# Gated layer's second output projection: both column pairs by seven block products, and the last head's root applied by a diagonal matrix in the transposition

## The chip, the core and the metric

The kernel runs on one core of a Trainium2 chip. The metric is the device time in microseconds (us) of one execution, of which the median over several runs is taken. The core has a matrix engine (TensorE: PE in the profile, PEld for its weight loads), VectorE (DVE), ScalarE (ACT), GpSimd (POOL), and a queue engine (SP) that starts most transfers from memory.

## The reference

Two layers with a gated feed path stand one after the other: a gated linear attention layer (4 heads, 1024 value columns each) and a retention layer (8 heads). There are 256 tokens, a model width of 2048 and an inner width of 4096, all in float32. What matters here is the end of the attention layer:

```
o = o * lax.rsqrt(jnp.mean(o * o, axis=-1, keepdims=True) + EPS)     # per token and head
o = o.reshape(B, S, D_INNER).astype(h.dtype) * head_g
return (o * jax.nn.silu(gate)) @ w_out                               # w_out: 4096 x 2048
h = h + gla_mixer(...)                                               # then the retention layer
```

## The kernel before

Every weight is float32 and comes from memory in blocks of 128 x 1024 (512 KB; two row tiles of 512 columns), into buffers called `raw`. A block is then split into two parts that the matrix engine multiplies at full rate: `hi`, a rounded copy made by ACT (L298), and `lo`, the remainder `raw - hi` made by DVE (L299). A product of a row tile of the block with 128 tokens is three matmuls of 512 columns: hi with hi, lo with hi, hi with the activations' lo part (`three`, L408; `mm3`, L341 to L343). There are four `hi` and four `lo` buffers (L203, L204), and a split is started at most three ahead of the one that PE works on (`LOOK = 3`). What is called a split below has a number in program order (lo216 is the 217th).

Where two groups of 512 output columns use the same left side, the kernel can compute both together for the first half of the rows (kt 0 to 7, for both halves of the tokens) by seven products of blocks in place of eight, in the manner of Strassen and Winograd: `pair` in `_plan` orders loads and splits, and `out_pair` (L985) does the arithmetic. The left sides of four of the products are sums of activations, made by `make_sums` (L441; tiles `osum`). The right sides are sums of weight blocks: some are made by a transfer that adds while it writes (POOL, L310), some by an addition on DVE (L293) just before a split. A product over 4 row tiles is two splits of 6 matmuls each (`product`, L418); the second half of the rows (kt 8 to 15) is done directly for both columns, in splits of 12 matmuls (`direct`, L425). Products `P1` to `P8` and the direct steps `v4` to `v7`, `g4` to `g7` follow one another in the order of a string such as `UNIT`. `JOINT` (L169) says for each projection which of its two pairs of columns are done this way: for the second half of this layer's projection, `("ao", 1)`, the first pair is not, and its two columns (tiles `gb0`, `gb1`) are 8 direct splits each; the second pair (tiles `gbe2`) is.

The left side of this projection, `ogt`, is written by `og_part` (L880) for each of a head's two groups of 512 columns: the head's root `hr` is formed from the sums of squares `sso` by a chain of small DVE instructions (`rsqrt`, Newton steps, L492 to L497), then `o`, `hr` and the gate `sg` are multiplied in one DVE instruction for 128 tokens (L895), `transpose_out` (L701) transposes 128 x 128 blocks by PE against the identity (L707; tiles `got6`, `got7` for the last head), and ACT and DVE split the transposed blocks into `ogt` (L500, L501). The last head (number 3, groups 6 and 7) fills kt 8 to 15 of this half. So kt 0 to 7 are there earlier.

The order of instructions on each engine is set by a scheduler when the program is built: it starts from the order in the code, from priorities (`high_priority`) and from what must stay in order (`keep`), and each engine then runs its list in order. Transfers are issued in order by SP (loads of `raw`) and POOL (adding transfers, and the residual `gb_resid`, 2 MB, L481).

Of the kernel before, what the change touches and what calls it, by code (L numbers as in the profile page):

```python
# [17 lines left out]
P = 128  # L18
# [46 lines left out]
def _plan():  # L65


    loads, subs = [], []

    def load(gid, j):  # L70
        loads.append((gid, j))
        return len(loads) - 1

    def use(c, pre=None, post=()):
        subs.append((c, pre, post))

    def plain(gid, js=range(NSUB)):
        for j in js:
            use(load(gid, j))

    def pair(g, v, q=None, order=None):
        order = (order or UNIT).split()
        x = [load(g, 0), load(g, 1)] if order[0] == "P1" else []
        z = []
        later = max(("P3", "P6"), key=order.index)
        for n, tok in enumerate(order):
            kind, i = tok[0], tok[1:]
            if kind in "qvg":
                plain({"q": q, "v": v, "g": g}[kind], [int(i)])
            elif tok == "z":  # L90
                z += [load(v, 2), load(v, 3)]
            elif tok == "P2":
                plain(g, [2, 3])
            else:
                if tok == "P1" and not x:
                    x += [load(g, 0), load(g, 1)]
                for j in range(2):
                    post = []
                    if tok == later:
                        post.append((z[j], (v, j)))  # L100
                    if tok == "P1":
                        post.append((x[j], (v, j)))
                    if tok == "P6":
                        post.append((x[j], (g, 2 + j)))
                    use(z[j] if tok in ("P3", "P7") else x[j], z[j] if tok == "P6" else None, post)

    def out_cols_of(name, half, cut, joint):
        for c in (0, 2):
            cols = [(name, half, c + n) for n in range(2)]
            if joint[c // 2]:  # L110
                pair(cols[1], cols[0])
# [36 lines left out]
    free = [-1 - n for n in range(NRAW)] + [-1] * len(SPARE)  # L148
    buf = []
    for c in range(len(loads)):  # L150
        b = min([*range(NRAW), *_spare(loads[c])], key=lambda n: free[n])
        buf.append(b)
        free[b] = last[c]
    return loads, subs, places, last, buf


UNIT = "P1 v4 z P3 v5 P5 v6 P6 P2 v7 P7 g4 g5 P8 g6 g7"
MIXED = "q0 q1 P1 q2 q3 q4 z P5 q5 P6 q6 q7 P2 P3 v4 v5 v6 P7 v7 g4 g5 P8 g6 g7"
WHOLE = " ".join(f"q{j}" for j in range(NSUB)) + " " + UNIT


def ret_order(h):
# [16 lines left out]
def kernel(  # L179
# [261 lines left out]
    def make_sums(lhs, name, where):  # L441
        s = cur["s"] = [None] * 4
# [12 lines left out]
        yield  # L455
        tt(f3, f6, y[1][:, :, one_], ALU.add)
        tt(f7, y[0][:, :, one_], y[0][:, :, two], ALU.subtract)
        yield
        for i, x in ((0, f3), (1, f5), (2, f6), (3, f7)):
            if i % 2 == 0:  # L460
                two_ = room(i // 2)
                s[i], s[i + 1] = two_[:, 0], two_[:, 1]
            keep(nc.scalar.activation(s[i][:, :, 0, :], x, AF.Copy))
            keep(tt(s[i][:, :, 1, :], x, s[i][:, :, 0, :].bitcast(F32), ALU.subtract))
            if i % 2:
                yield
# [234 lines left out]
    def transpose_out(src, kt0, scale0, dst, name):  # L701
        for half in range(2):
            tp = mis_p.tile([P, 2, SEQ], F32, tag="mis", name=f"{name}_tp{half}")
            for jj in range(2):
                j = half * 2 + jj
                for t in range(2):
                    nc.tensor.transpose(  # L707
                        tp[:, jj, t * P : (t + 1) * P], src(t, j), ident
                    )
            kt = kt0 + half * 2  # L710
            with tc.high_priority():
                if scale0 is None:
# [123 lines left out]
    def gla_head(h):  # L836
# [42 lines left out]

        def og_part(gj):  # L880
            g = 2 * h + gj
            if gj == 0:
# [9 lines left out]
            o, sg, hr = os_[gj], sgs[gj], hw["hr"]  # L892
            with tc.high_priority():
                for t in range(2):
                    nc.vector.scalar_tensor_tensor(  # L895
                        o[:, t, :], o[:, t, :], hr[:, t : t + 1], sg[:, t, :], ALU.mult, ALU.mult
                    )
            yield
            yield from transpose_out(
                lambda t, j: o[:, t, j * P : (j + 1) * P],  # L900
# [1 line left out]
                S_HG + 4 * g,  # L902
                ogt,
                f"got{g}",
            )
# [79 lines left out]
    def out_pair(c, first, name, final=False):  # L985
# [36 lines left out]
        g = c + 1  # L1022
        cur["pin"] = final
        product(A, plain(0, 0), stop=True)
        advance()
        direct(lhs, (C, V1), 4)
        join(g, 0, A)
        advance()
        product(C, summed(0))
        advance()  # L1030
        direct(lhs, (C, V1), 5)
        drain_side()
        product(P5, summed(1), stop=True)
        direct(lhs, (C, V1), 6)
        for t in range(2):
            join(c, t, P5)
        product(A, summed(2), stop=True)
        product(B, plain(4, 0))
        join(c, 0, A, ALU.subtract)
        direct(lhs, (C, V1), 7, stop=True)  # L1040
# [26 lines left out]
        if onward:  # L1067
            for _ in late[0]:
                pass
            tasks.append(out_transposes(g))  # L1070
        begun.clear()
        closed.clear()

# [24 lines left out]
    def out_half(first, final, name, cut=0, hook=None, joint=(False, False)):  # L1098
        pend = {}
        for c in range(4):  # L1100
            if joint[c // 2]:
                if c % 2 == 0:
                    out_pair(c, first, name)
                continue
            if cut and c == 0:
                if True:
# [353 lines left out]
    for h in range(2, 4):  # L1460
        gla_head(h)
    get_resid("gb_resid")
    slots = deque((2, 3, 0, 1))
    out_half(False, False, "gb", joint=JOINT["ao", 1])
    put_resid("resid_g")
# [122 lines left out]
```

## Time and profile before

| | |
|---|---|
| median of the three runs | 1374.34 us (1373.69 to 1375.95) |
| time of the profiled execution | 1373.26 us |
| its span, first to last instruction | 1371.5 us |
| PE busy | 1362.3 us, 99% of the span |
| DVE, ACT, POOL busy | 1098.4, 847.0, 136.8 us |
| the last head's group 7 gates end, the projection's first column pair starts | 565.1 us into the span |
| first column pair ends, second begins | 611.4 us |

The span is the time between the first and the last instruction; the execution's own time is 1.76 us longer. Durations below are those of this one execution. A busy time of PE counts each matmul from its start to its end, and matmuls overlap: two of 512 columns start 0.227 us apart and each shows 0.39 us. So waits of PE are read from the distances of the starts. DVE and ACT instructions overlap a little too (0.08 to 0.10 us), so that the distance of starts is again what one costs.

### The profile page before, as it was taken

To read this page: it belongs to the slowest core of one execution; us is meant where nothing else is said; L and a number is where in the kernel's file an instruction comes from. 1 tells how busy PE (TensorE), PEld (TensorE's weight loads), DVE (VectorE), ACT (ScalarE), POOL (GpSimd) and SP (SyncE) were. 2 spreads that over 40 slices of the span, in tenths; PEclk is the share of its full clock that TensorE was granted. 3 is DMA by queue.
4 is the path that set the end of the run, shared out by engine and by line. 5 is a ranking of instruction groups with operands and counts; after the bars stand their busy time and mean duration, and the time that the engine had idled before them with its cause. 6 is when DMAs were issued, how large, how long until landed. Compare 5 with 4: busy or idle time off the path is not lost.

```text
span 1371.5 us, 18372 instructions
## 1 busy us (share of the span) xinstructions
PE 1362.3 (99%) x6564; PEld 1145.0 (83%) x6564; DVE 1098.4 (80%) x1520; ACT 847.0 (62%) x1119; POOL 136.8 (10%) x194
## 2 busy tenths in 40 slices
PE   9999999999999999999999999999999999999997
PEld 8888888888888888888888888888888888888886
DVE  6686795987878896769887988897867897889796
ACT  6576656656567756656666576655546665666565
POOL 1003020110021021001011010100101101010010
PEclk9999999999999999999999999999999999999999
DMA  9755566789658667868897878796798797979773
GB/s 358 259 175 168 169 208 184 156 247 318 200 153 262 204 204 183 319 169 232 267 331 197 260 202 249 207 316 218 172 367 219 240 261 197 259 198 317 241 176 124
DMA packets 84508, 315.04 MB, mean 230 GB/s; under 512 B 9776, under 2 KB 10800, under 8 KB 83136
## 3 DMA queue, kind: packets, MB, share of 16 engines
q1 hardware_dynamic: 67200, 241.63, 50.4%
q0 software_dynamic: 15920, 64.89, 23.9%
q10 hardware_dynamic: 1296, 7.35, 1.4%
q8 instruction: 51, 0.84, 0.2%
q14 instruction: 41, 0.34, 0.1%
HBM read 303.35 MB, written 10.49 MB: 229 GB/s over the span
## 4 chain that ended last, share of the span: by engine, by line
PE 99%; DMA 1%; DVE 0%; ACT 0%; DVEq 0%; issue 0%; ACTq 0%
PE rqk_ps L384 8%; PE re_ps L412 8%; PE re_ps L413 8%; PE re_ps L414 8%; PE rqk_ps L385 4%; PE gqk_ps L384 4%; PE gg_ps L342 3%; PE gv_ps L343 3%; PE gv_ps L341 3%; PE gv_ps L342 3%; PE gg_ps L341 3%; PE gg_ps L343 3%; PE ge_ps L412 2%; PE ge_ps L413 2%; PE ge_ps L414 2%; PE gae_ps L413 2%
## 5 line engine op out<-in xcount | busy, mean ns | idle before, releaser
L299 DVE TENSOR_TENSOR lo<-raw,hi 128x1024 fp32r<-128x1024 f32 (+1 forms) x568 | 687.4, 1221 | 215.5 <-ACT hi L298 205.5
L298 ACT ACTIVATE hi<-raw 128x1024 fp32r<-128x1024 f32 (+1 forms) x568 | 595.9, 1055 | 394.3 <-DMA raw<-in_w_all 50.8
L384 PE MATMUL rqk_ps<-xhl,hi 128*128 128x512 f32 x480 | 162.9, 397 | 0.0
L413 PE MATMUL re_ps<-lo,xhl 128*128 128x512 f32 x352 | 137.5, 391 | 0.0
L414 PE MATMUL re_ps<-hi,xhl 128*128 128x512 f32 x352 | 137.3, 390 | 0.0
L310 POOL DMA_DIRECT2D raw<-in_w_all x90 | 78.0, 868 | 556.1 <-DVE lo L299 222.1
L412 PE MATMUL re_ps<-hi,xhl 128*128 128x512 f32 x352 | 132.6, 391 | 0.0
L385 PE MATMUL rqk_ps<-xhl,lo 128*128 128x256 f32 x480 | 122.5, 281 | 0.0
L384 PEld LDWEIGHTS rqk_ps<-xhl,hi 128*128 128x128 f32 x480 | 89.7, 188 | 17.8
L385 PEld LDWEIGHTS rqk_ps<-xhl,lo 128*128 128x128 f32 x480 | 87.6, 189 | 3.4
L414 PEld LDWEIGHTS re_ps<-hi,xhl 128*128 128x128 f32 x352 | 66.1, 188 | 13.6
L413 PEld LDWEIGHTS re_ps<-lo,xhl 128*128 128x128 f32 x352 | 66.2, 188 | 13.2
L412 PEld LDWEIGHTS re_ps<-hi,xhl 128*128 128x128 f32 x352 | 66.0, 188 | 13.2
L384 PE MATMUL gqk_ps<-xhl,hi 128*128 128x512 f32 x216 | 76.6, 399 | 0.0
L342 PE MATMUL gg_ps<-lo,xhl 128*128 128x512 f32 x192 | 75.5, 393 | 0.0
L342 PE MATMUL gv_ps<-lo,xhl 128*128 128x512 f32 x192 | 75.3, 392 | 0.0
L341 PE MATMUL gv_ps<-hi,xhl 128*128 128x512 f32 x192 | 75.2, 393 | 0.0
L343 PE MATMUL gv_ps<-hi,xhl 128*128 128x512 f32 x192 | 75.1, 391 | 0.0
L343 PE MATMUL gg_ps<-hi,xhl 128*128 128x512 f32 x192 | 75.0, 391 | 0.0
L341 PE MATMUL gg_ps<-hi,xhl 128*128 128x512 f32 x192 | 74.9, 392 | 0.0
L829 POOL TENSOR_TENSOR s<-s,m 128x64 f32<-128x64 f32 x56 | 36.1, 676 | 232.5 <-DVE m L820 223.2
L385 PE MATMUL gqk_ps<-xhl,lo 128*128 128x256 f32 x216 | 59.1, 281 | 0.0
(434 smaller groups left out, 2659.8 us busy)
## 6 DMA issues: line engine op xcount, KB each, us to landing
raw<-in_w_all SPq DMA_DIRECT2D x449, 512.0 KB, 4.9
raw<-in_w_all POOLq DMA_DIRECT2D x90, 512.0 KB, 6.8
resid<-in_x_n SPq DMA_DIRECT2D x2, 1024.0 KB, 10.8
gg<-in_gn_g POOLq DMA_DIRECT2D x8, 256.0 KB, 4.2
resid_x<-resid ACTq DMA_DIRECT2D x1, 2048.0 KB, 7.9
gb<-in_gn_b POOLq DMA_DIRECT2D x8, 256.0 KB, 6.0
gb_resid<-resid_x POOLq DMA_DIRECT2D x1, 2048.0 KB, 11.3
resid_g<-gb_resid ACTq DMA_DIRECT2D x1, 2048.0 KB, 10.5
```

Source lines behind the costliest of these rows:

```text
L298: a = nc.scalar.activation(hi[:, sl], src[:, sl], AF.Copy)
L299: b = nc.vector.tensor_tensor(lo[:, sl], src[:, sl], hi[:, sl].bitcast(F32), ALU.subtract)
L310: nc.gpsimd.dma_start(raws[n], block(key), accum_op=ALU.add)
L341: pin(mm(ps, xh, hi[:, q, :], start=kt == 0, stop=False, **onto))
L342: pin(mm(ps, xh, lo[:, q, :], start=False, stop=False, **onto))
L343: pin(mm(ps, xl, hi[:, q, :], start=False, stop=kt == end - 1, **onto))
L384: mm(ps[c], wh, rhs[:, kt, :, :], start=kt == 0, stop=False)
L385: mm(ps[c][:, 0, :], wl, rhs[:, kt, 0, :], start=False, stop=False)
L412: pin(mm(ps, xh, hi[:, q, :], start=start, stop=False, **again))
L413: pin(mm(ps, xh, lo[:, q, :], start=False, stop=False, **again))
L414: pin(mm(ps, xl, hi[:, q, :], start=False, stop=stop, **again))
L829: nc.gpsimd.tensor_tensor(dst, dst, side_of(m[:, li, :], z), ALU.add)
```

## The change

The first pair of columns of `("ao", 1)` is done by seven products as well (`JOINT`), in an order of its own, `LATE`, which puts products that need only kt 0 to 7 ahead of the direct steps. The sums of activations are made during the last head (`make_sums(..., "next_s")`, stepped in `joint_turn`). In the last head, `o` is multiplied by the gate alone, as soon as the gate is there; the root goes into two diagonal matrices `hd` (the identity with each row times `hr`, DVE), and the transposition becomes an ordinary float32 matmul of `o` with `hd`. `out_pair` gets a second order of steps (`late_direct`).

```
-    ("ao", 1): (False, True),
+    ("ao", 1): (True, True),
...
+LATE = "P1 P2 z P3 v4 P5 v5 P6 v6 v7 P7 g4 g5 P8 g6 g7"
...
-                    nc.tensor.transpose(
-                        tp[:, jj, t * P : (t + 1) * P], src(t, j), ident
-                    )
+                    to = tp[:, jj, t * P : (t + 1) * P]
+                    if diag is None:
+                        nc.tensor.transpose(to, src(t, j), ident)
+                    else:
+                        mm(to, src(t, j), diag[:, t, :], start=True, stop=True)
...
+            scaled = h == GLA_H - 1
+            if scaled and gj == 0:
+                hw["diag"] = sc_p.tile([P, 3, P], F32, tag="s32", name=f"hd{h}", bufs=1)
+            if scaled:
+                with tc.high_priority():
+                    for t in range(2):
+                        nc.vector.tensor_tensor(o[:, t, :], o[:, t, :], sg[:, t, :], ALU.mult)
...
+                    if scaled:
+                        for t in range(2):
+                            nc.vector.tensor_scalar(hw["diag"][:, t, :], ident, hr[:, t : t + 1], None, ALU.mult)
...
+        making = make_sums(ogt, "osum2", sums_in_v, "next_s") if h == 3 else None
...
+            if making and tok in ("P3", "P5", "P6", "v7", "g6"):
+                next(making)
...
         product(A, plain(0, 0), stop=True)
...
+        if late_direct:
+            product(B, plain(4, 0))
+            join(g, 0, A)
+            product(C, summed(0))
+            while len(side) > 1:
+                advance()
+            advance()
+            direct(lhs, (C, V1), 4)
+            advance()
+            product(P5, summed(1), stop=True)
+            advance()
+            direct(lhs, (C, V1), 5)
+            for t in range(2):
+                join(c, t, P5)
+            drain_side()
+            product(A, summed(2), stop=True)
+            direct(lhs, (C, V1), 6)
+            join(c, 0, A, ALU.subtract)
+            direct(lhs, (C, V1), 7, stop=True)
...
+                    out_pair(c, first, name, late_direct=c == 0 and name == "gb")
```

On DVE, in the first microseconds of the projection, the list before reads so (hr3 is the last head's root, go6 and go7 its two groups, lo219 to lo221 are the splits of direct steps 3 to 5 of the first column):

```order
L497 SCALAR_TENSOR_TENSOR hr3_4993<-hr3_nw_4996 128x2
L895 SCALAR_TENSOR_TENSOR go6_4710<-go6_4710,hr3_4993,gsg6_4650 128x512 x2
L895 SCALAR_TENSOR_TENSOR go7_4945<-go7_4945,hr3_4993,gsg7_4654 128x512
L299 TENSOR_TENSOR lo219_5038<-raw187_4844,hi219_5037 128x1024
L895 SCALAR_TENSOR_TENSOR go7_4945<-go7_4945,hr3_4993,gsg7_4654 128x512
L299 TENSOR_TENSOR lo220_5065<-raw188_4856,hi220_5064 128x1024
L299 TENSOR_TENSOR lo221_5092<-raw189_4877,hi221_5091 128x1024
L501 SCALAR_TENSOR_TENSOR ogt_106<-got6_tp0_5053,smalls_102,ogt_106 128x256
L501 SCALAR_TENSOR_TENSOR ogt_106<-got6_tp1_5080,smalls_102,ogt_106 128x256
```

and at the same place now, from the join of the first product to the splits of P6 (hd3 are the diagonal matrices; raw184 += raw188 and raw185 += raw189 are the weight sums for splits 226 and 227):

```order
L1018 TENSOR_TENSOR gb_resid_5056<-gbe0_ps1_5059,gb_resid_5056 128x512
L497 TENSOR_TENSOR hr3_nw_5021<-hr3_nw_5021 128x2
L300 TENSOR_TENSOR lo223_5110<-raw184_4824,hi223_5109 128x1024
L300 TENSOR_TENSOR lo224_5121<-raw185_4826,hi224_5120 128x1024
L498 SCALAR_TENSOR_TENSOR hr3_5018<-hr3_nw_5021 128x2
L300 TENSOR_TENSOR lo225_5161<-raw191_4965,hi225_5160 128x1024
L294 TENSOR_TENSOR raw184_4824<-raw184_4824,raw188_4866 128x1024
L294 TENSOR_TENSOR raw185_4826<-raw185_4826,raw189_4892 128x1024
L903 TENSOR_SCALAR hd3_4990<-ident_103,hr3_5018 128x128 x2
L300 TENSOR_TENSOR lo226_5188<-raw184_4824,hi226_5187 128x1024
L300 TENSOR_TENSOR lo227_5200<-raw185_4826,hi227_5199 128x1024
```

The multiplication of go6 and go7 has gone up the list (go6 into the seven products of group 7), the diagonals stand behind two splits of the weights and two additions, and the splits 226 and 227 behind them.

On PE, the transpositions of group 6 stood within the third direct split of column 0 (tiles gb0):

```order
L341 MATMUL gb0_ps1_5034<-hi218_5010,ogt_106 128x512
L342 MATMUL gb0_ps1_5034<-lo218_5011,ogt_106 128x512
L707 MATMUL got6_tp0_5053<-ident_103,go6_4710 128x128
L707 MATMUL got6_tp1_5080<-ident_103,go6_4710 128x128
L343 MATMUL gb0_ps1_5034<-hi218_5010,ogt_106 128x512
L707 MATMUL got6_tp0_5053<-ident_103,go6_4710 128x128 x3
L707 MATMUL got6_tp1_5080<-ident_103,go6_4710 128x128 x3
L341 MATMUL gb0_ps0_5033<-hi218_5010,ogt_106 128x512
L342 MATMUL gb0_ps0_5033<-lo218_5011,ogt_106 128x512
L343 MATMUL gb0_ps0_5033<-hi218_5010,ogt_106 128x512
```

and stand now behind four products, within the first split of `P6` (lo226; tile gbe0_p5 is the bank of `P5`):

```order
L414 MATMUL gbe0_p5_5062<-lo224_5121,osum20_4883 128x512
L415 MATMUL gbe0_p5_5062<-hi224_5120,osum20_4883 128x512
L413 MATMUL gbe0_ps1_5059<-hi226_5187,osum21_5012 128x512
L712 MATMUL got6_tp0_5130<-hd3_4990,go6_4710 128x128
L712 MATMUL got6_tp1_5139<-hd3_4990,go6_4710 128x128
L712 MATMUL got6_tp0_5130<-hd3_4990,go6_4710 128x128 x3
L712 MATMUL got6_tp1_5139<-hd3_4990,go6_4710 128x128 x3
L414 MATMUL gbe0_ps1_5059<-lo226_5188,osum21_5012 128x512
L415 MATMUL gbe0_ps1_5059<-hi226_5187,osum21_5012 128x512
L413 MATMUL gbe0_ps1_5059<-hi226_5187,osum21_5012 128x512
```

PE's list now has P1, P2, P3, P5 and one matmul of P6 ahead of the first transposition, 49 matmuls, where 29 of the projection stood before; the direct step v4 (split 222) comes only behind split 227's first matmul.

On POOL, the transfers that add weight blocks followed on the residual's load for the second pair only (raw200 to raw204):

```order
L481 DMA gb_resid_5031<-resid_x_2994 128x4096
L310 DMA raw200_5163<-in_w_all 128x1024
L310 DMA raw201_5181<-in_w_all 128x1024
L310 DMA raw203_5225<-in_w_all 128x1024
L310 DMA raw204_5252<-in_w_all 128x1024
L310 DMA raw200_5163<-in_w_all 128x1024
L310 DMA raw201_5181<-in_w_all 128x1024
```

and now come for both pairs; raw184 and raw185 are written again for `P5`, raw188 and raw189 for `P7`, raw184 and raw185 once more for `P8`:

```order
L482 DMA gb_resid_5056<-resid_x_2994 128x4096
L311 DMA raw184_4824<-in_w_all 128x1024
L311 DMA raw185_4826<-in_w_all 128x1024
L311 DMA raw188_4866<-in_w_all 128x1024
L311 DMA raw189_4892<-in_w_all 128x1024
L311 DMA raw184_4824<-in_w_all 128x1024
L311 DMA raw185_4826<-in_w_all 128x1024
```

Six adding transfers are new on POOL, and SP has two loads fewer (448 for 450). In all there are 576 splits for 570.

More of the change, by code (lines that the diff above doesn't have):

```diff
@@ L110, in out_cols_of @@
             if joint[c // 2]:
-                pair(cols[1], cols[0])
+                pair(cols[1], cols[0], order=LATE if cols[0] == ("ao", 1, 0) else None)
                 continue
@@ L439, in sums_in_v, with make_sums @@
         return lambda n: v_p.tile([P, 2, QK, 2, P], F32R, tag="v", name=f"{name}{n}")
-    def make_sums(lhs, name, where):
-        s = cur["s"] = [None] * 4
+    def make_sums(lhs, name, where, key="s"):
+        s = cur[key] = [None] * 4
         room = where(name)
@@ L699, in o_mms, with transpose_out @@
                 mm(ps[t], al, v[:, s, 0, :], start=False, stop=end)
-    def transpose_out(src, kt0, scale0, dst, name):
+    def transpose_out(src, kt0, scale0, dst, name, diag=None):
         for half in range(2):
@@ L881, in og_part @@
             g = 2 * h + gj
+            o, sg = os_[gj], sgs[gj]
+            scaled = h == GLA_H - 1
[5 more added lines that the diff above has]
+                        nc.vector.tensor_tensor(o[:, t, :], o[:, t, :], sg[:, t, :], ALU.mult)
             if gj == 0:
@@ L889, in og_part @@
                     rsqrt(hr, m, 2, f"hr{h}")
+                    if scaled:
+                        for t in range(2):
+                            nc.vector.tensor_scalar(hw["diag"][:, t, :], ident, hr[:, t : t + 1], None, ALU.mult)
                 hw["hr"] = hr
                 yield
[L892 to L897, printed above, removed]
+            hr = hw["hr"]
+            if not scaled:
+                with tc.high_priority():
+                    for t in range(2):
+                        nc.vector.scalar_tensor_tensor(
+                            o[:, t, :], o[:, t, :], hr[:, t : t + 1], sg[:, t, :], ALU.mult, ALU.mult
+                        )
             yield
@@ L983, in tail_banks, with out_pair @@
         return ps
-    def out_pair(c, first, name, final=False):
+    def out_pair(c, first, name, final=False, late_direct=False):
         lhs, s = ogt, cur["s"]
@@ L1024, in out_pair @@
         product(A, plain(0, 0), stop=True)
[L1025 to L1040, printed above, removed]
+        if late_direct:
[10 more added lines that the diff above has]
+            direct(lhs, (C, V1), 5)
+            for t in range(2):
+                join(c, t, P5)
[4 more added lines that the diff above has]
+            direct(lhs, (C, V1), 7, stop=True)
+        else:
+            advance()
+            direct(lhs, (C, V1), 4)
+            join(g, 0, A)
+            advance()
+            product(C, summed(0))
+            advance()
+            direct(lhs, (C, V1), 5)
+            drain_side()
+            product(P5, summed(1), stop=True)
+            direct(lhs, (C, V1), 6)
+            for t in range(2):
+                join(c, t, P5)
+            product(A, summed(2), stop=True)
+            product(B, plain(4, 0))
+            join(c, 0, A, ALU.subtract)
+            direct(lhs, (C, V1), 7, stop=True)
         product(A, summed(3), stop=True)
@@ L1069, in out_pair @@
                 pass
-            tasks.append(out_transposes(g))
+            (side if c == 0 else tasks).append(out_transposes(g))
         begun.clear()
@@ L1102, in out_half @@
                 if c % 2 == 0:
-                    out_pair(c, first, name)
+                    out_pair(c, first, name, late_direct=c == 0 and name == "gb")
                 continue
@@ L1462 @@
     get_resid("gb_resid")
+    cur["s"] = cur["next_s"]
     slots = deque((2, 3, 0, 1))
```

1 line of the change is left out of this document (added).

## The prediction

> **What bounds the kernel now.** I read the page first: span, busy shares, the chain that ended last.
>
> ```profile
> span 1371.5 us, 18372 instructions
> ...
> PE 1362.3 (99%) x6564; PEld 1145.0 (83%) x6564; DVE 1098.4 (80%) x1520; ACT 847.0 (62%) x1119; POOL 136.8 (10%) x194
> ...
> PE 99%; DMA 1%; DVE 0%; ACT 0%; DVEq 0%; issue 0%; ACTq 0%
> ```
>
> PE is the chain. A busy share of 99% could hide short waits, since matmuls overlap, so the view of waits comes second. These are all that PE has in the whole span:
>
> ```profile
> PE warm_ps L521 <- POOL lnone L523: 1.0, 1, 1.0
> PE zps L640 <- DVE wa L614: 0.4, 1, 0.4
> ```
>
> Both are at the start. So a change can gain only what it takes out of PE's list, and loses whatever it makes PE wait. Third, the stretches around the first column pair, in columns PE, PEld, DVE, ACT, POOL, clock, DMA share, GB/s:
>
> ```profile
> 560.00:570.00 10.00, 10.00 (x46) 8.29 (x45) 9.23 (x22) 6.10 (x9) 0.00 (x0) 1.00 0.85 346
> 570.00:580.00 10.00, 10.00 (x51) 8.30 (x51) 6.66 (x9) 5.00 (x8) 0.00 (x0) 1.00 0.71 212
> 580.00:590.00 10.00, 10.00 (x47) 8.32 (x46) 4.62 (x7) 4.62 (x7) 0.00 (x0) 1.00 0.53 159
> 590.00:600.00 10.00, 10.00 (x49) 8.34 (x49) 7.86 (x10) 6.86 (x12) 0.00 (x0) 1.00 0.60 194
> ```
>
> DVE is 92% busy in the first ten microseconds and then has room: that is the pattern to keep in mind, since a pair by products asks DVE for more, and earliest.
>
> **PE's list: minus 12 matmuls, 16 dearer transpositions.** The first and the 28th of the projection's matmuls in order of time:
>
> ```profile
> 565.06 0.39 PE L341 MATMUL gb_ps<-hi,ogt 128*128 128x512 f32 x1
> 571.18 0.39 PE L341 MATMUL gb_ps<-hi,ogt 128*128 128x512 f32 x1
> ```
>
> 27 steps in 6.12 us are 0.2267 us a matmul. Two columns directly are 16 splits of 12, 192 matmuls; the pair by products is 14 splits of 6 and 8 of 12, 180. That is 12 x 0.2267 = 2.72 us less.
>
> A transposition is one matmul; the float32 product with the diagonal I price by the float32 products of the same shape in the score stage, two records each (4 heads x 7 levels x 2 products are 56, the trace has 112). Rows of the chain, and the group:
>
> ```profile
> 92.54 1.34 PE lv L763 x12
> 153.65 0.87 PE got_tp L707 x8
> L763 PE MATMUL lv<-w 128*128 128x128 f32 x112 | 15.7, 274 | 0.0
> ```
>
> 0.112 us a record, so 0.223 us a product, against 0.109 for a transposition: 16 x 0.114 = 1.83 us more. PE's list gets shorter by 0.89 us, and that is the most that the change can gain with these prices.
>
> [...] The trace's rows put the ratio at 2, and I take the rows.
>
> **The waits: DVE's list from split 218 to P6.** DVE before, in order of time:
>
> ```profile
> 563.64 1.23 DVE L299 TENSOR_TENSOR lo<-raw,hi 128x1024 fp32r<-128x1024 f32 x1 [0.29 <-ACT hi L298]
> 564.78 0.15 DVE L496 TENSOR_TENSOR hr_nw<-hr_nw 128x2 f32<-128x2 f32 x1
> 564.85 0.68 DVE L1401 TENSOR_TENSOR gsg<-ge_ps,gsg 128x512 f32<-128x512 f32 x1
> 565.45 0.15 DVE L497 SCALAR_TENSOR_TENSOR hr_nw<-hr_nw 128x2 f32<-128x2 f32 x1
> 565.63 0.16 DVE L495 SCALAR_TENSOR_TENSOR hr_nw<-hr_nw,hm 128x2 f32<-128x2 f32 x1
> ...
> 566.22 2.08 DVE L895 SCALAR_TENSOR_TENSOR go<-go,hr,gsg 128x512 f32<-128x512 f32 x3
> 568.22 1.22 DVE L299 TENSOR_TENSOR lo<-raw,hi 128x1024 fp32r<-128x1024 f32 x1
> ```
>
> By the distances of starts a split costs DVE 1.14 us, a 128x512 operation 0.60, a small step 0.07 between long ones and 0.18 behind one that it depends on. A direct split feeds PE for 12 x 0.2267 = 2.72 us, a split of a product for 1.36. So in a run of products DVE has 0.22 us beside each split, and the new list puts far more there. ACT before:
>
> ```profile
> 562.54 1.06 ACT L298 ACTIVATE hi<-raw 128x1024 fp32r<-128x1024 f32 x1 [0.78 <-PE ge_ps L414]
> 565.26 0.69 ACT L1403 ACTIVATE gsg<-ge_ps,rr 128x512 f32<-128x512 f32 x1 [1.66 <-PE ge_ps L414]
> 565.85 1.05 ACT L298 ACTIVATE hi<-raw 128x1024 fp32r<-128x1024 f32 x1
> ```
>
> Split 218 waits for its `hi` and that for PE, as before: I start it at 563.64 again. From there to the first weight addition's end the new list has: eight splits (218 to 225), 8 x 1.14 = 9.12; the gate sum and the two products of go7, 3 x 0.60 = 1.80; the join of P1, 0.60; ten small steps, 0.8; the first product of go7 waits for the gate (565.95 by ACT's row, where DVE is ready at 565.5), 0.5; the addition raw184 += raw188, at its full length by this row:
>
> ```profile
> L293 DVE TENSOR_TENSOR raw<-raw,raw 128x1024 f32<-128x1024 f32 x30 | 36.3, 1221 | 0.1
> L663 DVE TENSOR_SCALAR dg<-ident,rr x2: 283/284/284, 55.3 to 55.5; 128x128 f32<-128x128 f32 x2
> ```
>
> Together 14.0 us, so it ends at 577.7. Then ACT makes hi226 (1.06): 578.8. PE would be there after eight splits of products, 565.06 + 8 x 1.36 = 575.9: **2.9 us of waiting**. A first part shows earlier: lo223 ends at 563.64 + 5 x 1.14 + 3.6 (the other work ahead of it) + 1.23 = 574.2, and PE wants it at 573.4, so about 0.8 falls ahead of P5 and 2.1 ahead of P6. The transpositions wait for the diagonals: the second addition starts at 577.6, the diagonals (second row above, 0.2 apart, 0.28 long) end at 579.2, where PE stands at 579.0: 0.2 us more. The sum of waits is 3.1 us. The transpositions and the rest of split 226 then take 2.9 us, in which lo227 (done at 581.5) comes in time; from there direct steps of 2.72 us a split follow, four of them (v4 to v7), and DVE regains its lead.
>
> What I cost at nothing, with its cover: the four splits of `osum` on ACT and DVE (0.5 and 0.6 us each) fall before 563, where ACT shows 0.78 us of idleness just ahead of hi218 and both wait for PE; without cover they would push split 218 back by up to 1.2. Six more splits, one more addition pair, five more joins make 6 x 1.14 + 2 x 1.14 + 5 x 0.60 = 12 us on DVE; in the four stretches above it idles 11.6, so what does not lie in the first 14 us fits into the later stretches and those behind them. Two loads fewer on SP and six adding transfers on POOL are 2 MB more in a stretch whose DMA share is 0.53 to 0.85.
>
> Sum: -2.72 + 1.83 + 3.1 = **+2.2 us**. The profiled execution took 1373.26 us, 1.08 under the median of the runs; on the median's footing 1374.34 + 2.2 = 1376.5. The unknown price is the wait. Its bounds: none (the list's order hides it, as the view of waits has it for the second pair before, which runs the same products) and, where the adding transfers are late as well, 6.3.
>
> **The rivals.** No change that a measurement tells is within 0.2% of 1374 us, 2.75 us either way; the forecast lies inside, near the slow edge.
>
> *The adding transfers are late (slower).* Split 223 and 224 read raw184 and raw185 after an adding transfer on POOL, which starts when lo216 and lo217 are done (the first row below, two splits: 560.5 and 561.7), just as the residual's 2 MB leave the same queue. Landing times of an adding transfer in this kernel, alone and as the fourth of a burst, and the residual's:
>
> ```profile
> 559.29 2.41 DVE L299 TENSOR_TENSOR lo<-raw,hi 128x1024 fp32r<-128x1024 f32 x2 [0.33 <-ACT hi L298]
> ```
>
> ```profile
> raw<-in_w_all POOLq DMA_DIRECT2D x1, 512.0 KB, 5.5
> raw<-in_w_all POOLq DMA_DIRECT2D x1, 512.0 KB, 11.9
> gb_resid<-resid_x POOLq DMA_DIRECT2D x1, 2048.0 KB, 11.3
> raw<-in_w_all SPq DMA_DIRECT2D x1, 512.0 KB, 14.5
> ```
>
> hi224 has to start by 573.0, so raw185 may take 11.3 us. At 5.5 nothing happens; at 11.9 it adds 0.6, at 14.5 (a plain load that lay behind the residual) 3.2: 1379.7. That is the point from which it decides. Against it: only two stand in the queue, not four.
>
> *PE's clock falls (slower).* PE starts the kernel at half rate:
>
> ```profile
> 3.72 1.92 PE L521 MATMUL warm_ps<-warm 128*128 128x128 f32 x8
> 5.29 1.72 PE L372 MATMUL gqk_ps<-xhl,hi 128*128 128x512 f32 x4
> 7.32 1.08 PE L372 MATMUL gqk_ps<-xhl,hi 128*128 128x512 f32 x4
> ```
>
> Eight records in 1.92 us where later 12 take 1.34, four matmuls in 1.72 where the next four take 1.08: 1.0 + 0.6 us lost. If the wait ahead of P6 brought that back, the sum would be +3.8: 1378.1. [...]
>
> *No wait (not slower).* If DVE's list runs ahead, because PE comes later to it than I count, or the waits are only 0 to 1 us, the sum is -0.9 to 0: 1373.4 to 1374.3. For it: in the second pair before, PE shows no wait at all. Against it: there direct steps lie between products, and no root, gate or diagonal is in DVE's list.
>
> *Faster.* Beyond -0.9 us the transpositions would have to cost what they did, 1374.34 - 2.72 = 1371.6.
>
> **How the numbers follow.** The forecast has 0.50, its own range 1375.0 to 1378.0 (a wait of 1.6 to 4.6); late transfers 0.20; the clock or dearer transpositions 0.07; no wait 0.20; faster 0.03. Slower by over 0.2% (above 1377.1) are the two slow rivals and a third of the forecast: 0.27 + 0.17 = 0.44. Faster 0.03, within 0.53. The range leaves out the lower half of "no wait" and "faster" (0.13) and two of these rivals at once (0.05), and reaches to the dearest of them: 1373.8 to 1379.9.
>
> **What would show it.** The view of waits should have PE waiting at the projection's first pair, some 0.8 us for lo223 (P5) and 2 for hi226 (P6), and DVE without idleness for 14 us ahead of it. PE should show 180 matmuls on the first pair's tiles, and transpositions with two records each, 0.11 apart. The second pair should start about 2 us later than at 611.4. The prediction is wrong if hi223 or hi224 wait for a transfer, if the waits come elsewhere (ahead of split 219, for the gate; ahead of P7, for raw188 and raw189), or if there are none.

## The result and the profile after

The changed kernel takes 1377.5 us (median of 22 runs, 1375.22 to 1378.92) where the kernel before takes 1373.91 (22 runs beside it). The ratio is 1.0023, with an interval of 1.0017 to 1.0029: 3.6 us slower. The profiled execution of the changed kernel took 1376.97 us. Its page, the span, TensorE's part and the chain that ended last:

```profile
span 1375.2 us, 18426 instructions
PE 1363.1 (99%) x6568; PEld 1144.6 (83%) x6568; DVE 1109.8 (81%) x1535; ACT 853.5 (62%) x1126; POOL 142.2 (10%) x200
PE 95%; issue 2%; DMA 1%; DVE 1%; ACT 0%; POOL 0%; DVEq 0%; POOLq 0%; ACTq 0%
```

TensorE shows four records more than before: 12 matmuls less and 16 second records of the products with the diagonal. Its share of the chain has fallen from 99% to 95%. That is not 4% of waiting: followed back from the end, the chain leaves TensorE at the wait ahead of P6 and comes back to it only at 526.5 us, and the 52 us between lie on ACT, DVE, POOL and transfers. Two of the four waits of PE, in us, times and longest (the others are the two at the start, as before):

```profile
PE gbe_ps L413 <- ACT hi L299: 2.1, 1, 2.1
...
PE gbe_p L414 <- DVE lo L300: 0.7, 1, 0.7
```

Both are new. The same stretch in order of time, with start and length; gbe_ps and gbe_p are the first pair's banks, gbe_p that of P5. The first and the last row are the first matmuls of the first and of the second pair:

```profile
564.15 0.39 PE L413 MATMUL gbe_ps<-hi,ogt 128*128 128x512 f32 x1
...
572.32 0.39 PE L413 MATMUL gbe_p<-hi,osum 128*128 128x512 f32 x1
573.40 0.50 PE L414 MATMUL gbe_p<-lo,osum 128*128 128x512 f32 x1 [0.70 <-DVE lo L300]
573.74 0.39 PE L415 MATMUL gbe_p<-hi,osum 128*128 128x512 f32 x1
...
574.66 0.40 PE L413 MATMUL gbe_p<-hi,osum 128*128 128x512 f32 x1
575.14 0.50 PE L414 MATMUL gbe_p<-lo,osum 128*128 128x512 f32 x1
575.48 0.40 PE L415 MATMUL gbe_p<-hi,osum 128*128 128x512 f32 x1
...
576.17 0.40 PE L415 MATMUL gbe_p<-hi,osum 128*128 128x512 f32 x1
578.65 0.80 PE L413 MATMUL gbe_ps<-hi,osum 128*128 128x512 f32 x1 [2.08 <-ACT hi L299]
579.24 3.25 PE L712 MATMUL got_tp<-hd,go 128*128 128x128 f32 x16
582.24 0.47 PE L414 MATMUL gbe_ps<-lo,osum 128*128 128x512 f32 x1
...
587.09 1.05 PE L712 MATMUL got_tp<-hd,go 128*128 128x128 f32 x8
...
614.77 0.39 PE L413 MATMUL gbe_ps<-hi,ogt 128*128 128x512 f32 x1
```

The pair takes 614.77 - 564.15 = 50.62 us. Before it took from 565.06 to 611.4, 46.3: 4.3 us more, of which the rest of the span gives back 0.6.

By the distances of starts, less 0.23 for a matmul, TensorE waits 0.85 + 0.11 us ahead of P5 (split 223), 0.25 + 0.11 within P5 (split 224) and 2.25 ahead of P6 (hi226): 3.57 us. Then there is something that no view of waits lists: the first 16 records of the transpositions take 3.0 us to the start of the next matmul (579.24 to 582.24), the 8 at 587.09 only 0.8. The view by stretches (columns PE, PEld, DVE, ACT, POOL, granted clock, DMA share, GB/s), cut where the granted clock changes, says why:

```profile
575.14:578.55 3.41, 1.43 (x5) 0.86 (x5) 3.41 (x5) 1.01 (x1) 0.59 (x1) 1.00 0.35 82
578.55:581.96 3.41, 3.31 (x14) 3.22 (x15) 2.67 (x5) 1.45 (x3) 2.48 (x4) 0.50 0.88 173
581.96:585.37 3.41, 3.41 (x19) 2.90 (x18) 1.93 (x4) 2.39 (x5) 0.42 (x1) 1.00 1.07 199
```

For 3.41 us behind the wait the clock is at one half, which costs half of that, 1.7 us. So the terms are -2.72 (12 matmuls), +1.76 (16 x 0.11 for the second records), +3.57 (waits) and +1.7 (half clock): 4.3, what the pair shows.

DVE and ACT in the same stretch (DVE first, then ACT):

```profile
563.11 1.23 DVE L300 TENSOR_TENSOR lo<-raw,hi 128x1024 fp32r<-128x1024 f32 x1
...
572.13 1.22 DVE L300 TENSOR_TENSOR lo<-raw,hi 128x1024 fp32r<-128x1024 f32 x1
573.86 1.23 DVE L300 TENSOR_TENSOR lo<-raw,hi 128x1024 fp32r<-128x1024 f32 x1 [0.51 <-ACT hi L299]
...
576.21 2.35 DVE L294 TENSOR_TENSOR raw<-raw,raw 128x1024 f32<-128x1024 f32 x2
578.48 0.48 DVE L903 TENSOR_SCALAR hd<-ident,hr 128x128 f32<-128x128 f32 x2
```

```profile
572.77 2.01 ACT L299 ACTIVATE hi<-raw 128x1024 fp32r<-128x1024 f32 x2 [1.91 <-DMA raw<-in_w_all]
577.54 2.19 ACT L299 ACTIVATE hi<-raw 128x1024 fp32r<-128x1024 f32 x2 [2.76 <-DVE raw L294]
```

And POOL's issues of the two adding transfers for P5, raw184 and raw185:

```profile
560.50 0.86 POOL L311 DMA_DIRECT2D raw<-in_w_all  x1 [10.96 <-DVE lo L300]
561.64 0.85 POOL L311 DMA_DIRECT2D raw<-in_w_all  x1 [0.27 <-DVE lo L300]
```

DVE starts split 218 at 563.11 and is busy to the end of the first addition at 577.4 with one hole of 0.5 us, in which ACT waits for the transfer of raw185. That transfer was issued at 561.64 and is read from 572.77 on; the chain goes through it, but what it adds is this hole of 0.5 us, as the run without it shows below. ACT makes hi226 behind the addition, from 577.54 to 578.60, and TensorE goes on at 578.65.

### The profile page after: what moved, and what is told of

Its sections match the earlier page's. It is cut to its first block, busy times and chain, and to the rows that moved or that the text cites. A ratio compares the mean times of both kernels' runs of the same rounds, so it can differ in the third digit from the quotient of the medians.

```text
span 1375.2 us, 18426 instructions
## 1 busy us (share of the span) xinstructions
PE 1363.1 (99%) x6568; PEld 1144.6 (83%) x6568; DVE 1109.8 (81%) x1535; ACT 853.5 (62%) x1126; POOL 142.2 (10%) x200
## 4 chain that ended last, share of the span: by engine, by line
PE 95%; issue 2%; DMA 1%; DVE 1%; ACT 0%; POOL 0%; DVEq 0%; POOLq 0%; ACTq 0%
PE rqk_ps L385 8%; PE re_ps L413 8%; PE re_ps L415 8%; PE re_ps L414 8%; PE rqk_ps L386 4%; PE gqk_ps L385 4%; PE gg_ps L343 3%; PE gv_ps L344 3%; PE gv_ps L343 3%; PE gv_ps L342 3%; PE gg_ps L344 3%; PE gg_ps L342 3%; PE gae_ps L414 2%; PE gae_ps L415 2%; PE gae_ps L413 2%
## 5 line engine op out<-in xcount | busy, mean ns | idle before, releaser
L311 POOL DMA_DIRECT2D raw<-in_w_all x96 | 83.3, 869 | 556.1 <-DVE lo L300 308.0
```

The source lines that it names most:

```text
L311: nc.gpsimd.dma_start(raws[n], block(key), accum_op=ALU.add)
```

## The experiments

Ratios are to the kernel before, run beside each group on the same chip. Its median was 1373.93 us for the first four kernels, 1373.72 for the next four and 1373.84 for the last two.

### The diagonal alone

```
-    ("ao", 1): (True, True),
+    ("ao", 1): (False, True),
-        making = make_sums(ogt, "osum2", sums_in_v, "next_s") if h == 3 else None
+        making = None
-    cur["s"] = cur["next_s"]
```

> The kernel before with the diagonal alone: the first pair of columns stays direct, the sums of activations are not made early, the root of the last head goes through the transposition. Theory (a product with the diagonal is two records of 0.11 us, no wait): 16 x 0.112 us more on TensorE, +1.8 us, about 1375.7 where the kernel before has 1373.9. [...] If the records of the products are 0.21 us apart here too, the spacing of the changed kernel's first twelve isn't the clock's.

1375.68 us, ratio 1.0012 (1.0003 to 1.0021): 1.75 us more by the medians, 0.4 to 2.9 by the interval. TensorE has no wait in this part of the kernel, and all 32 records are of the short kind (busy time, mean ns):

```profile
L712 PE MATMUL got_tp<-hd,go 128*128 128x128 f32 x32 | 4.0, 274 | 0.0
```

In the changed kernel the same group is 5.3 us and 332 ns. So a product costs two records, and the slow records there are not its price: the first pair's stretch is 1.75 us longer than before (564.77 to 612.82, where 46.3 us were).

### The pair alone

```
-            scaled = h == GLA_H - 1
+            scaled = False
```

> The changed kernel with the root back in the multiplication of o and gate, and transpositions against the identity; the first pair stays in products in the same order of splits. Theory (the loss lies in DVE's list ahead of P5 and P6, the diagonal costs 1.8 us of its own): the list of TensorE is 2.7 us shorter, waits of 2 to 3 us remain in other places since the four multiplications of 0.6 us now lie ahead of split 223; 1373.2 to 1374.8. Rival (the diagonal alone is the loss): no waits, 1371.2.

1373.99 us, ratio 1.0006 (0.9997 to 1.0015): not to be told from the kernel before, though TensorE's list is 2.7 us shorter. The waits moved to other places, as DVE's rows explain (the four multiplications by root and gate stand ahead of split 223):

```profile
571.99 2.73 DVE L910 SCALAR_TENSOR_TENSOR go<-go,hr,gsg 128x512 f32<-128x512 f32 x4
574.64 2.35 DVE L300 TENSOR_TENSOR lo<-raw,hi 128x1024 fp32r<-128x1024 f32 x2
```

```profile
574.11 0.87 PE L710 MATMUL got_tp<-ident,go 128*128 128x128 f32 x6 [0.79 <-DVE go L910]
575.23 0.50 PE L413 MATMUL gbe_ps<-hi,ogt 128*128 128x512 f32 x1 [0.24 <-ACT ogt L501]
581.27 0.50 PE L413 MATMUL gbe_ps<-hi,osum 128*128 128x512 f32 x1 [0.96 <-ACT hi L299]
```

By the distances of starts these are 2.9 us. -2.72 + 2.9 is 0.2; measured 0.06. The diagonal isn't the only loss: without it, the pair by products earns nothing.

### Matmuls in the wait ahead of P6

```
             product(P5, summed(1), stop=True)
+            for n in range(8):
+                mm(A, lhs[:, 0, 0, 0:P], splits[state["sub"]][1][:, n % 2, :], start=True, stop=True)
             advance()
             direct(lhs, (C, V1), 5)
```

> The changed kernel with 8 matmuls of 512 columns put between P5 and P6, into a bank that P6 then overwrites; they read the split ready last before P6, so they run in the wait for hi226. Theory (the wait costs 2.1 us itself and another 1.7 us because TensorE runs at half clock for 3.4 us behind it): the wait shrinks from 2.1 to about 0.3 with the end of it unmoved, the granted clock stays at 1.00 and the transpositions are 0.11 us a record: 1375.8 where the changed kernel has 1377.5. Rival (the slow transpositions are slow by themselves, or the clock falls all the same): 1377.5.

The bank is the one of P1, onto which P6 adds; one column group is so computed from something else; the number and the shapes of the other instructions stay. TensorE:

```profile
576.63 2.01 PE L1056 MATMUL gbe_ps<-lo,ogt 128*128 128x512 f32 x8
578.73 0.50 PE L413 MATMUL gbe_ps<-hi,osum 128*128 128x512 f32 x1
579.07 1.95 PE L712 MATMUL got_tp<-hd,go 128*128 128x128 f32 x16
```

The wait ends at 578.73, 13.97 us behind the pair's first matmul (564.76), where it ended 14.50 us behind it (578.65 and 564.15), though 1.8 us of matmuls were put in: what it waits for isn't TensorE's own. The clock stays at 1.00 (575.00 to 582.00), and 16 records take 1.95 us in place of 3.25. The time is 1376.22 us, ratio 1.0018 (1.0009 to 1.0027): 1.3 us less than the changed kernel by the distances to the kernel before, where 1.7 were expected. The intervals of the two overlap; it is the profile that shows the half clock gone. There the pair takes 48.57 us (to 613.33), 2.05 less than in the changed kernel: the second wait within P5 (0.36) is not there this time, and 1.7 are left, which is the price of the half clock by its length.

### Three matmuls in place of eight

This edit is against the kernel with eight.

```
-            for n in range(8):
+            for n in range(3):
```

> As the kernel with 8 matmuls between P5 and P6, with 3 of them (they write over the bank that holds P1, onto which P6 adds, so that one column group is left wrong; the 8 did so too). They take 0.7 us of the wait of 2.1 us; 1.4 us are left. Theory: the end of the wait doesn't move. If the half clock needs more idle time than that, 1375.8 as with 8; if it comes at 1.4 us too, 1377.5, with 3.4 us of half clock in the profile.

```profile
579.53 0.50 PE L413 MATMUL gbe_ps<-hi,osum 128*128 128x512 f32 x1 [1.31 <-ACT hi L299]
579.86 1.95 PE L712 MATMUL got_tp<-hd,go 128*128 128x128 f32 x16
```

1376.26 us, ratio 1.0019 (1.0009 to 1.0028), the time of the kernel with eight. A wait of 1.5 us by starts is left, and the clock doesn't fall (1.00 from 577.74 to 584.56). The waits with the three matmuls are 3.24 us by starts, and -2.72 + 1.76 + 3.24 is 2.28; the pair takes 48.60 us (565.49 to 614.09), 2.3 more than before. So without the half clock the terms close.

### Without the additions

```
                 added.add(n)
-                nc.vector.tensor_tensor(raws[at], raws[at], raws[by], ALU.add)
+                if loads[at][0] != ("ao", 1, 1):
+                    nc.vector.tensor_tensor(raws[at], raws[at], raws[by], ALU.add)
```

> The changed kernel without the two additions of weight blocks on DVE for P6 of the first pair (raw184 += raw188, raw185 += raw189 are left out, so that the first pair's columns are computed from other weights). Theory (DVE's list sets the wait ahead of P6): the list is 2.3 us shorter there, the wait for hi226 goes, those ahead of P5 stay (0.9 and 0.25 us), the clock doesn't fall: 3.7 us less, 1373.8. Rival (P6 waits for a buffer or a transfer): the wait of 2.1 us stays and 1377.5 with it.

```profile
575.52 0.50 PE L415 MATMUL gbe_p<-lo,osum 128*128 128x512 f32 x1 [0.69 <-DVE lo L301]
...
578.14 0.46 PE L414 MATMUL gbe_ps<-hi,osum 128*128 128x512 f32 x1
578.44 1.95 PE L713 MATMUL got_tp<-hd,go 128*128 128x128 f32 x16
```

The wait for hi226 is gone (578.14 follows 577.92), the one ahead of P5 stands, and the clock stays up: the 16 records take 1.95 us, and the mean granted clock of this execution is 0.999. 1374.47 us, ratio 1.0005 (0.9996 to 1.0014), 3.1 us less than the changed kernel by the distances where 3.7 were expected. So the 2.25 us and the half clock behind them come from the end of DVE's list, not from a buffer or a transfer.

### Splits in the order of their use

```
-LATE = "P1 P2 z P3 v4 P5 v5 P6 v6 v7 P7 g4 g5 P8 g6 g7"
+LATE = "P1 P2 z P3 P5 P6 v4 v5 v6 v7 P7 g4 g5 P8 g6 g7"
...
             product(C, summed(0))
+            product(P5, summed(1), stop=True)
...
+            product(A, summed(2), stop=True)
+            advance()
             direct(lhs, (C, V1), 4)
```

A line that is not shown makes an addition no earlier than behind the last split that still reads its block.

> The changed kernel with the first pair's weights split in the order in which TensorE uses them: P1 P2 P3 P5 P6 and then v4 to v7, so that the splits of v4 and v5 no longer stand ahead of those of P5 and P6. Theory (all that DVE does ahead of P5 and P6 adds to the waits): the first wait ahead of P5 (0.9 us) goes, that for the late transfer grows (raw185 lands at 572.7, P5's second split would be used from 573.9 on), and the additions end 2.3 us earlier at most; waits of 2.0 to 2.9 us in all where there were 3.7, and the clock falls or not: 1374.8 to 1377.0. Rival (the order of the splits doesn't matter, since the additions and the diagonal come behind the transfer): 1377.5.

1376.55 us, ratio 1.0022 (1.0012 to 1.0031), within the bounds, but not for the reason expected. TensorE's waits:

```profile
575.62 0.50 PE L414 MATMUL gbe_p<-lo,osum 128*128 128x512 f32 x1 [0.57 <-DVE lo L300]
577.92 0.50 PE L413 MATMUL gbe_ps<-hi,osum 128*128 128x512 f32 x1 [0.88 <-ACT hi L299]
586.43 1.13 PE L712 MATMUL got_tp<-hd,go 128*128 128x128 f32 x8 [0.97 <-DVE ogt L502]
```

With a fourth of 0.3 they sum to 3.5 us by starts, as much as in the changed kernel. What the splits of v4 and v5 no longer took ahead of P6 came back where group 7's transpositions wait for DVE to empty group 6's. What the kernel gains is that the clock stays up: its longest wait at this pair is 1.0 us in the view of waits, the 16 records take 1.95 us, and the mean granted clock of this execution is 0.999. -2.72 + 1.76 + 3.5 = +2.6, measured +2.8.

### Without the transfers for P5

```
         for n, key in post:
+            if loads[n][0] == ("ao", 1, 1) and key[0] == ("ao", 1, 0):
+                continue
             nc.gpsimd.dma_start(raws[n], block(key), accum_op=ALU.add)
```

> The changed kernel without the two adding transfers for P5 of the first pair (raw184 and raw185 are not written again, so that P5 is computed from other weights). Theory (the transfer of raw185 lands 2 us after ACT would have read it and leaves a hole of 0.5 us in DVE's list): the second wait ahead of P5 (0.25 us) and the hole go, the wait for hi226 is about 0.3 us shorter, waits fall by 0.5 us: 1377.0. Rival (late transfers are what P5 and P6 wait for): all waits go, 1373.8.

1377.33 us, ratio 1.0027 (1.0016 to 1.0039), where 1377.0 was expected: next to nothing is gained. P5 is computed from other weights here, with the same instructions but for the two transfers. The small wait within P5 is gone (it is not in the profile with eight matmuls either, where the transfers are), and hi226 is waited for 2.0 us in place of 2.25. DVE has no hole from split 223 on: from split 218 (565.42) to the end of the first addition (579.3) it needs 13.9 us, where the changed kernel needed 14.3. So the wait is that of DVE's list, and the transfer adds 0.4 us. The clock still falls, to 0.50 at 581.84, when TensorE has been at work again and was busy for 1.55 of the last 3.41 us:

```profile
578.43:581.84 3.41, 1.55 (x12) 1.32 (x11) 3.41 (x5) 2.12 (x2) 1.73 (x2) 1.00 0.67 163
581.84:585.25 3.41, 3.41 (x14) 3.02 (x13) 2.52 (x5) 1.31 (x3) 1.74 (x2) 0.50 0.89 174
```

### Direct steps first, halves of the rows exchanged

```
+FLIP = "v4 v5 v6 v7 g4 g5 P1 P2 z P3 g6 P5 g7 P6 P7 P8"
...
+        f = lambda j: (j + flip) % NSUB
...
-    ("ao", 1): (False, True),
+    ("ao", 1): (True, True),
...
+            G1 = lev_p.tile([P, GW], F32, tag="lev", name=f"{name}e{c}_g1")
+            for j in range(4, 8):
+                direct_((C, V1), j, stop=j == 7)
...
+            making = make_sums(ogt, "osum", sums_in_v, 2 * flip)
```

The edit is against the kernel before.

> The kernel before (root in the multiplication, transpositions against the identity) with both pairs by seven products, but with the two halves of the rows exchanged: the direct steps are those of kt 0 to 7, which need nothing of the last head, and six of the eight come first, two columns at a time into four banks and a fifth from the pool of P5; the products are those of kt 8 to 15, and the sums of activations are made during the direct steps. Theory (the loss is DVE's overload in the first 14 us, where each split feeds TensorE for 1.36 us only): splits of direct steps feed it for 2.72 us, so DVE has the time for root, transposed blocks and sums; the list is 2.7 us shorter with no wait, 1371.2. Rival (DVE is late again, with the sums ahead of P3 or the additions behind): waits of 2 us or more, 1373.2 or more.

1388.14 us, ratio 1.0104 (1.0089 to 1.0119). The rival held, and more than it said. TensorE waits 2.4 us for split 228, which DVE reaches late among the sums, and 8.4 us ahead of P7. There P6, P7 and P8 stand without a direct step between them, and the transfers that add weights for P7 and P8 are not there yet. P7 itself waits for the subtraction of P6's product from the residual, which stands in DVE's list behind the splits 235 and 236 (P7's second, P8's first). Behind both waits TensorE goes at half its pace for a while: its matmuls start 0.43 us apart from 594.84 to 597.82, where they start 0.23 apart ahead of the first wait and from 598.18 on, and the two at 617.07 and 617.63 last 0.77 and 0.63 us where others last 0.39. The mean granted clock of this execution is 0.994. ACT's rows for these two:

```profile
610.22 1.06 ACT L301 ACTIVATE hi<-raw 128x1024 fp32r<-128x1024 f32 x1 [5.72 <-DMA raw<-in_w_all]
613.42 1.06 ACT L301 ACTIVATE hi<-raw 128x1024 fp32r<-128x1024 f32 x1 [2.14 <-DMA raw<-in_w_all]
```

### A transfer in place of the additions, order held

```
-LATE = "P1 P2 z P3 v4 P5 v5 P6 v6 v7 P7 g4 g5 P8 g6 g7"
+LATE = "P1 P2 z P3 P5 v4 v5 v6 P6 v7 P7 g4 g5 P8 g6 g7"
...
+                    if tok == "P5" and order == LATE.split():
+                        post.append((x[j], (v, 2 + j)))
...
+            cur["pin"] = True
             product(B, plain(4, 0))
```

A line that is not shown drops the additions. The same was run with the root in the multiplication (`scaled = False`) and with the diagonal.

> Both pairs by seven products, the root in the multiplication as before, the first pair's order P1 P2 P3 P5 v4 v5 v6 P6 v7 with TensorE's matmuls held in that order, and the weight sums for P6 made by an adding transfer behind P5's splits in place of the additions on DVE. Theory (DVE's list decides): 2.3 us of additions and the splits of v4 and v5 no longer stand ahead of P6, but the four multiplications by root and gate (2.6 us) stand ahead of split 223, P5's second: a wait of 1.5 to 2.5 us ahead of it, none ahead of P6; list 2.7 us shorter: 1372.7 to 1373.9 where the kernel before has 1373.8. Rival (the transfers for P6 are late in place of the additions): 2 us or more of waiting for hi227, 1375 or more.

> The same order with the diagonal: the two multiplications of o by the gate stay early, and the transpositions stand behind P5. Theory: no wait ahead of P5 but the one for the transfer (1 us at most); the diagonals stand behind split 226 in DVE's list, which waits for a buffer that P5's first half frees, so TensorE waits 1.5 to 2 us for them behind P5; list 0.9 us shorter: 1374.3 to 1376.0. Rival (the wait goes with the additions): 1373.0.

1383.18 us (ratio 1.0065, 1.0053 to 1.0078) and 1386.71 us (1.0090, 1.0075 to 1.0105), both far above what was expected. The waits within P5 and for the diagonals are there (0.95 us by starts in the first kernel, less than expected; 2.4 in the second), but a longer one follows in both. In the first, TensorE and ACT:

```profile
587.34 1.94 PE L712 MATMUL got_tp<-ident,go 128*128 128x128 f32 x8 [8.17 <-DVE ogt L504]
```

```profile
583.29 1.06 ACT L301 ACTIVATE hi<-raw 128x1024 fp32r<-128x1024 f32 x1 [4.18 <-DMA raw<-in_w_all]
584.26 0.82 ACT L503 ACTIVATE ogt<-got_tp,smalls 128x256 fp32r<-128x256 f32 x2
```

The split of P6 stands in ACT's list ahead of the second half of group 6's transposed blocks. It waits 4.2 us for the transfer that took the addition's place, and with it the blocks wait, and with them group 7's transpositions and v4, whose split had long been made. The first kernel's rival had seen the late transfer, but not what stands behind it. In the second kernel the clock is at 0.50 for 10.2 us as well (584.69 to 594.93); in the first the eight transpositions at 587.34 take 1.94 us where the eight at 576.01 take 1.03. The mean granted clock of both executions is 0.994.

None of these versions beats the kernel before.

## Why the prediction was right, and where its sizes were off

The time, 1377.5, lies in the range and in the forecast's own range. The change is +3.6 us where +2.2 was forecast: the wait on DVE's list, on which the forecast rested, is there, and a term that it left to a rival came on top in part of the executions. The second pair was to start about 2 us later than at 611.4 and started at 614.77. Step by step:

- *TensorE's list.* 12 matmuls less are in the counts. The transpositions were put at +1.83 and took 1.75 us alone. The trace's ratio of two held. The top of the range, 1379.9, and a part of the 0.07 hold a dearer price of these products, which no run shows; what the run with the diagonal alone showed in its place is the 1.75 us.
- *DVE's list from split 218 to P6.* This step held most closely: the first addition was to end at 577.7 and ended at 577.4, hi226 was to be ready at 578.8 and was at 578.6. Waits of 0.8 and 2.1 us were named for lo223 and hi226; the view of waits has 0.7 and 2.1, the starts 0.96 and 2.25. From split 218 to the end of the first addition DVE needed 14.3 us where 14.0 were counted: the 0.5 us for the gate did not come, and 0.5 us went to the transfer of raw185; it began 0.5 us earlier. That these misses cancel is luck. The run without the additions shows the cause.
- *The diagonals.* The 0.2 us for them did not come: they were done at 578.96, before TensorE reached its transpositions.
- *The adding transfers.* raw185 was to be there within 11.3 us and could be read after 11.1 (561.64 to 572.77). Still, one of the signs named against the prediction showed: hi224 did wait for its transfer (1.91 us of ACT, 0.5 of them a hole on DVE). In this profile that cost 0.36 us within P5 and up to 0.5 ahead of P6, and removing the transfers did not make the kernel faster. As a rival for the forecast it fell.
- *PE's clock falls.* This is where the forecast's sum failed. That a wait ahead of P6 would bring back the half clock of the kernel's start stood there as a rival, priced at 1.6 us (+3.8, 1378.1), with 0.07 for it and the dearer transpositions together. It happened, and its price in the profile is 1.7 us. Its low weight rested on no run: in the kernel before, PE's only waits are the two at the start. The changed kernel's trace has half clock behind a wait of 2.25 us. By the mean granted clock the half clock doesn't come in every execution. 3.41 us at one half are 0.0012 of the mean clock. The mean granted clock of the 22 runs is 0.997 in nine, all of them at 1376.97 us or more (median 1377.82, +3.9); the other thirteen have a median of 1376.20, +2.3. None of the 42 runs of the four kernels with a shorter wait ahead of P6 (eight matmuls, three, no additions, the other order) has 0.997. So the forecast's sum fits the executions that by this number keep the clock, the rival's those that lose it, and the median of +3.6 is a mixture. The last 4.76 us of the changed kernel's span, with TensorE idle, are at 0.50 too (3.1 us in the kernel before), so three digits don't sort each single run.
- *No wait; faster.* Both fell. Even the pair without the diagonal waits as long as its shorter list saves.

What stays open is whether the pair by products can be had without the waits. Of the three other orders that were tried for it, the splits in the order of their use lost a little less (+2.8 us) and the other two much more (+9 to +14), through adding transfers or DVE's list; an order that gives DVE its time and the transfers theirs was not found.

## What to carry to other kernels

An engine at 80% over the whole kernel can have nothing left in the 14 us where a change puts its work (here DVE, busy but for 0.5 us of 14.3): write out that engine's list from the last thing it waits for to the first thing that waits for it, with the durations of the trace, and compare its end with that of the list of the engine that waits. On a TensorE that is otherwise always busy, a wait of 2.25 us cost nearly twice its length here, through the clock (1.7 us more in the profile); several short ones cost only themselves (3.5 us in the run with the other order). And an addition that is moved from an engine to a transfer may stop more than it frees, because what stands behind the waiting instruction in its engine's list waits too (with the order held and the root in the multiplication, ACT waited 4.18 us for the transfer, and TensorE 8.17 for what stood behind).

## What the runs showed of the hardware

The traces show when the clock was at one half, not what sets the moment. In the changed kernel it is 0.50 from 578.55 to 581.96, 3.41 us, and 1.00 in the 3.41 us on either side; without the transfers it is 0.50 in the 3.41 us from 581.84 on; in the second of the two with the order held it is 0.50 from 584.69 to 594.93. Rows of the view by stretches of that length, for the kernel with three matmuls and for the second of the two with the order held:

```profile
577.74:581.15 3.41, 2.10 (x16) 1.67 (x15) 3.41 (x6) 2.11 (x2) 1.76 (x2) 1.00 0.69 171
581.15:584.56 3.41, 3.41 (x19) 2.93 (x19) 2.65 (x5) 2.85 (x5) 1.72 (x2) 1.00 0.95 180
```

```profile
577.86:581.28 3.42, 2.00 (x16) 1.86 (x16) 1.56 (x4) 0.00 (x0) 0.00 (x0) 1.00 1.06 213
581.28:584.69 3.41, 0.05 (x1) 0.00 (x0) 0.00 (x0) 0.74 (x1) 0.00 (x0) 1.00 1.03 281
584.69:588.10 3.41, 0.00 (x0) 0.00 (x0) 3.06 (x5) 1.25 (x4) 0.87 (x1) 0.50 0.80 305
588.10:591.51 3.41, 2.49 (x12) 2.52 (x12) 1.02 (x3) 1.05 (x3) 0.00 (x0) 0.50 0.96 167
```

In the 3.41 us ahead of the fall TensorE was busy for 1.43 us in the changed kernel, for 1.55 without the transfers and for 0.05 in the second of the two with the order held. In the first row of the kernel with three matmuls it was busy for 2.10 and in the first row of the other for 2.00, and in the next row the clock is still at 1.00. The last row is at half clock with 2.49 us busy, and the 3.42 us that follow (591.51 to 594.93) are at 0.50 too. With the halves exchanged the matmuls get slow at 594.84, 1.1 us after a wait of 2.4 us has ended (593.74). These are single stretches: a bound, of the wait or of the busy time, is not shown by them, nor is why only some executions lose the clock.
